# Rotary's quarter swap by ScalarE copies, and x's first block ahead of the other launch loads, in a two-layer decoder trunk

## The chip, the core and the metric

One core of a Trainium2 chip runs the whole program. The metric is device time in microseconds of one execution; the times shown are medians of several executions. TensorE (PE in the views) multiplies, VectorE (DVE) and ScalarE (ACT) do the elementwise work, GpSimd (POOL) some small steps, SyncE (SP) issues most loads. ScalarE and POOL issue DMAs too, in the order of their own instructions.

## The reference

Two layers; each is a token mixer and a gated feed-forward block, both between norms. The mixer has four mLSTM heads and eight attention heads over two key/value heads, 512 positions, window 128. The parts that the change touches are the first norm and the rotary embedding of q and k:

```python
def rmsnorm(x, g):
    xf = x.astype(jnp.float32)
    y = xf * lax.rsqrt(jnp.mean(xf * xf, axis=-1, keepdims=True) + EPS)
    return (y * g.astype(jnp.float32)).astype(x.dtype)

def rope(x):
    ...
    x1, x2 = xf[..., :D // 2], xf[..., D // 2:]
    return jnp.concatenate([x1 * cos - x2 * sin, x2 * cos + x1 * sin], axis=-1)

def reference(...):
    for l in range(DEPTH):
        h = rmsnorm(x, g_pre_mix[l])
        y = token_mixer(h, ...)
        x = x + rmsnorm(y, g_post_mix[l])
        h = rmsnorm(x, g_pre_ffn[l])
        y = conv_ffn(h, ...)
        x = x + rmsnorm(y, g_post_ffn[l])
```

## The kernel before

x is held as four blocks of 128 positions by 1024 channels. Every matrix operand is split into a rounded high part and the rest (`wsplit` L105 and L107 for weights: ScalarE copies the high part, VectorE subtracts; `split_evac` L120 and L121 for results), and each product is three TensorE products (`mm3`, L115).

**Launch.** The first block of x (`xload`, L154) and the constants `cs` with the identity (L656) and weights are issued on SyncE's queue, gb (the norm's gain, one row sent to all 128 partitions, L158) on ScalarE's. `prenorm_a` squares a block on ScalarE with a sum (L166), POOL makes the scale factor (L169, L170), VectorE applies it in two halves (L175). `prenorm_b` transposes the eight 128x128 pieces on TensorE (L183), and ScalarE and VectorE evacuate them, split (L188, L190). `head` then begins the products with the first weights (wta, four units). Engine order at the launch is held by hand: the first weight's split follows the Square of block 0 (`sq[0]`), the second's the evacuation of block 0 (`ev[0]`), the Square of block 1 the same evacuation.

**Attention stage.** Nine channel blocks of 128 (`zchan`, weights wch) are computed channel-major, 24 products each, in the order 4 (k), 1 and 0 (q of the first key/value head, two pairs of heads), 5 (mLSTM), 2 and 3 (q of the second), 6, 7, 8 (mLSTM). "Pair j" below is q's block j. For k and the four q blocks `rotary` runs when the block's PSUM bank is full: ScalarE copies the bank (L364), four DMAs on ScalarE's queue (L368) swap neighbouring quarters of 32 rows, VectorE multiplies the bank by the cosines (L370) and the swapped tile by the sines (`finish`, L373), then adds and splits (L399, L120, L121; for k L389). A `finish` runs inside the next channel block. The mLSTM blocks run a convolution of several VectorE steps (L412, L416).

Between these products, as a `Filler`, run the attention steps for eight pairs of query block and key/value head: scores (`att1`, L470, two PSUM banks), mask and maximum on VectorE (L476, L477, L480), exponentials on ScalarE (L484, L489), normalisation on VectorE (L491 to L493); the transposes of the result (`att2`, L499, one bank), evacuated with a mask by VectorE (L502); the products with v (`att3`, L513). There are four such banks ("aux") and four of "acc". A scheduler of the framework puts the instructions of every engine in one fixed order, by its own estimate of times; each engine works in that order. So a changed duration in the program's text also moves instructions elsewhere.

Of the kernel before, what the change touches and what calls it, by code (L numbers as in the profile page):

```python
# [10 lines left out]
BF16 = mybir.dt.bfloat16  # L11
U16 = mybir.dt.uint16
AF = mybir.ActivationFunctionType
ALU = mybir.AluOpType
# [8 lines left out]

GF = (8, 3, 4, 6)
START = 36
MF = (3, 2, 3, 3, 2)
EPS = 1e-6
NEG = -1e30
# [23 lines left out]
def tile_hymba_trunk(ctx: ExitStack, tc, x, wch, wta, wtb, wout, wup, wdn, par, gv, mhg, cst, rope, out):  # L52
    nc = tc.nc
    NOSYNC = mybir.DependencyInfo(mybir.DependencyClass.NoSync, mybir.DependencyReason.DATA)

    def after(ins, prev):
        if prev is not None:
            tc.add_manual_dep(ins.ins, prev.ins.name, NOSYNC, reason="slots")
        return ins
# [7 lines left out]
    wk = ctx.enter_context(tc.tile_pool(name="wk", bufs=10))  # L67
# [20 lines left out]
    def work(dt=F32):  # L88
        return wk.tile([128, WRK], dt, tag="wk", name=nm("wk"))

    def psum():
        return pp.tile([128, 512], F32, tag="aux", name=nm("aux"))
# [4 lines left out]
    def small(n, tag):  # L97
        return sp.tile([128, n], F32, tag=tag, name=nm(tag), bufs=1 if n >= 16 else 4)
# [52 lines left out]
    xs = [keep.tile([128, D], F32, name=f"x{c}") for c in range(NT)]  # L151

    def xload(c, eng=nc.sync):
        eng.dma_start(xs[c], x[c * 128:(c + 1) * 128, :])  # L154

    def gload(l, i, eng=None, gate=None):
        g = gbp.tile([128, D], F32, tag="gb", name=nm("gb"))
        after((eng or nc.gpsimd).dma_start(g, gv[l, i:i + 1, :].to_broadcast([128, D])), gate)  # L158
        return g

    sq, st, ev = {}, {}, {}

    def prenorm_a(c, gb, gate=None):
        junk = wk.tile([128, 1024], BF16, tag="wk", name=nm("junk"))
        ss = small(1, "ss")
        sq[c] = nc.scalar.activation(junk, xs[c], AF.Square, scale=1.0 / 32, accum_out=ss)  # L166
        after(sq[c], gate)
        rs = small(1, "rs")
        nc.gpsimd.tensor_scalar(rs, ss, EPS, None, ALU.add)  # L169
        nc.gpsimd.tensor_tensor(rs, rs, neghalf[:, 0:1], ALU.pow)  # L170
        hs = []
        for hf in range(2):
            h = work()
            sl = slice(hf * 512, hf * 512 + 512)
            st[c] = nc.vector.scalar_tensor_tensor(h[:, :512], xs[c][:, sl], rs, gb[:, sl], ALU.mult, ALU.mult)  # L175
            hs.append(h)
        return hs
# [182 lines left out]


    def rotary(y, ps, outs):
        r0 = work()
        nc.scalar.activation(r0[:, :512], ps, AF.Copy)  # L364
        r1 = work()
        for b in range(4):
            s = (b ^ 1) * 32
            nc.scalar.dma_start(r1[b * 32:b * 32 + 32, :512], r0[s:s + 32, :512])  # L368
        o = work()
        nc.vector.tensor_tensor(o[:, :512], ps, y.rcos, ALU.mult)  # L370

        def finish():
            nc.vector.tensor_tensor(r1[:, :512], r1[:, :512], y.rsin, ALU.mult)  # L373
            outs(o, r1)
        return finish
# [275 lines left out]

    hT = new_hT(hp)
    hs = {}
    xload(0)
    gb = gload(0, 0, nc.scalar)
    nc.sync.dma_start(cs, cst[:, 0:C_K])  # L656
    hs[0] = prenorm_a(0, gb)
    uA = head_weights(0, (0,), sq[0], st[0])
    prenorm_b(0, hs[0], hT)
    uA += head_weights(0, (1,), ev[0][0], ev[0][1])  # L660
# [22 lines left out]
    for l in range(L):  # L683
# [9 lines left out]
        for i in range(len(its) + 3):  # L693
# [9 lines left out]
            if 0 <= i - 3 < len(its) and its[i - 3][0] % 2:  # L703
                b, kv = its[i - 3]
# [65 lines left out]
        for hf in range(2):  # L770
            for n0 in range(0, 3):
                ps, w = first[seq[n0]]
# [5 lines left out]
        for i in range(2 * NK2):  # L778
            us = []
            for j in (i, i + 2 * NK2):  # L780
                if j in first:
                    ps = first[j][0]
                else:
                    w = upw(j)
                    ps = acc()
# [3 lines left out]
            s = work()  # L789
# [7 lines left out]
            _, lastg = split_evac(s[:, :512], o[0], o[1])  # L797
# [12 lines left out]
        for hf in range(2):  # L810
            if hf:
                banks[1] = [psum() for _ in range(NT)]
            for k2 in range(NK2 - (NTAIL if hf else 0)):
                w, _ = wsplit(wdn[l, hf, k2], 1024, wp)
# [3 lines left out]
        for k2 in range(NK2 - NTAIL, NK2):  # L818
            w, gate = wsplit(wdn[l, 1, k2], 1024, gp, lastg)
# [90 lines left out]
```

## Time and profile before

| | |
|---|---|
| median of 3 runs | 1131.44 us (1131.03 to 1133.36) |
| the profiled execution | 1130.86 us |
| its span, first to last instruction | 1129.1 us |
| TensorE busy | 1108.7 us, 98% |
| VectorE, ScalarE, POOL busy | 659.4, 455.9, 46.7 us |
| DMA | 111.07 MB, mean 98 GB/s |
| chain that ended last, by engine | TensorE 91%, VectorE 2%, DMA 1%, ScalarE 1% |

The span is what the traced instructions take; the execution's own time has 1.8 us more around it. A TensorE instruction's end is modelled, so TensorE's waits are read from the time lines, where a bracket gives the idle time before a row and what ended it.

### The profile page before, as it was taken

Reading aid. Unit: us, or ns where it says so; the run is one execution under the profiler, and the core shown is the slowest. Engines: PE = TensorE matmul, PEld = TensorE weight load, DVE = VectorE, ACT = ScalarE, POOL = GpSimd, SP = SyncE. Lnnn points to the kernel's source line nnn. Section 1 sums busy time; section 2 is a strip of 40 time slices with the busy share of each in tenths; the row PEclk is TensorE's granted clock in tenths of the full one; section 3 lists DMA queues with packets and bytes.
Section 4 is the critical chain, followed back from the end, with each engine's and each line's share of the span. In section 5 each row is a group of like instructions: output and inputs, shape, how many; then the busy total and the mean of one; then the engine's idle time right before and its main releaser. Section 6 shows DMA issues by size and latency. Waiting matters only on the chain.

```text
span 1129.1 us, 14371 instructions
## 1 busy us (share of the span) xinstructions
PE 1108.7 (98%) x5504; PEld 921.1 (82%) x5504; DVE 659.4 (58%) x1094; ACT 455.9 (40%) x882; POOL 46.7 (4%) x106
## 2 busy tenths in 40 slices
PE   6999999999999999999999999999999999999997
PEld 6877788988888888888897777889888888888886
DVE  5588775566666565223557887566566655652223
ACT  5454563444334443223354445444443334431221
POOL 2000011100000000000100000110000000000001
PEclk9999999999999999999999999999999999999999
DMA  7331440233333332334223215202222333233322
GB/s 265 110 98 45 145 135 13 89 112 93 95 101 104 93 93 93 98 108 127 81 93 107 77 62 187 75 19 90 98 94 93 96 102 102 94 93 93 97 90 74
DMA packets 33171, 111.07 MB, mean 98 GB/s; under 512 B 4192, under 2 KB 4352, under 8 KB 33104
## 3 DMA queue, kind: packets, MB, share of 16 engines
q1 hardware_dynamic: 29808, 102.98, 28.7%
q0 software_dynamic: 1232, 4.04, 1.1%
q10 hardware_dynamic: 2064, 3.15, 1.0%
q8 instruction: 43, 0.70, 0.3%
q14 instruction: 24, 0.20, 0.1%
HBM read 104.91 MB, written 2.10 MB: 95 GB/s over the span
## 4 chain that ended last, share of the span: by engine, by line
PE 91%; DVE 2%; DMA 1%; ACT 1%; issue 0%; ACTq 0%; DVEq 0%; POOLq 0%; POOL 0%
PE acc L115 74%; PE aux L115 11%; PE aux L513 1%; DMA wk<-wk 1%; PE aux L183 1%; PE aux L470 1%; PE aux L569 1%; PE aux L499 1%; PE aux L549 0%; DVE wk L412 0%; DVE w L107 0%; DMA raw<-in_wout_dram 0%; ACT wk L484 0%; PE aux L605 0%; PE aux L627 0%
## 5 line engine op out<-in xcount | busy, mean ns | idle before, releaser
L115 PE MATMUL acc<-g,w 128*128 128x512 f32 (+1 forms) x2256 | 482.0, 376 | 0.0
L115 PEld LDWEIGHTS acc<-g,w 128*128 128x128 f32 x2256 | 404.2, 188 | 76.7
L107 DVE TENSOR_TENSOR w<-raw,w 128x1024 fp32r<-128x1024 f32 (+2 forms) x162 | 192.8, 1191 | 267.6 <-ACT w L105 267.5
L105 ACT ACTIVATE w<-raw 128x1024 fp32r<-128x1024 f32 (+2 forms) x162 | 167.7, 1035 | 336.9 <-PE acc L115 294.7
L115 PE MATMUL acc<-w,h 128*128 128x384 f32 (+2 forms) x672 | 146.1, 364 | 0.7 <-DVE h L190 0.5
L648 DVE SCALAR_TENSOR_TENSOR wk<-acc,par,wk 128x511 f32<-128x511 f32 (+1 forms) x176 | 131.3, 746 | 3.0
L115 PEld LDWEIGHTS acc<-w,h 128*128 128x128 f32 x672 | 118.7, 190 | 17.2 <-issue 4.8
L115 PE MATMUL acc<-h,w 128*128 128x512 f32 x432 | 106.4, 398 | 0.0
L115 PEld LDWEIGHTS acc<-h,w 128*128 128x128 f32 x432 | 78.9, 188 | 18.2 <-issue 1.5
L115 PE MATMUL acc<-w,g 128*128 128x512 f32 x384 | 88.7, 389 | 0.0
L115 PEld LDWEIGHTS acc<-w,g 128*128 128x128 f32 x384 | 72.1, 188 | 15.0
L646 ACT ACTIVATE wk<-acc,par 128x512 f32<-128x512 f32 x88 | 58.9, 669 | 0.0
L115 PE MATMUL aux<-g,g 128*128 128x512 f32 x240 | 55.0, 389 | 0.0
L120 ACT ACTIVATE g<-wk 128x512 fp32r<-128x512 f32 x36 | 22.8, 633 | 76.3 <-DVE wk L791 68.3
L115 PEld LDWEIGHTS aux<-g,g 128*128 128x128 f32 x240 | 45.0, 188 | 9.3
L115 PE MATMUL acc<-h,g 128*128 128x512 f32 x192 | 45.2, 393 | 0.1
L115 PE MATMUL aux<-w,h 128*128 128x512 f32 x192 | 43.8, 389 | 0.0
L115 PEld LDWEIGHTS aux<-w,h 128*128 128x128 f32 x192 | 36.0, 188 | 7.5
L115 PEld LDWEIGHTS acc<-h,g 128*128 128x128 f32 x192 | 35.6, 188 | 7.7 <-ACT g L120 0.5
L175 DVE SCALAR_TENSOR_TENSOR wk<-x,rs,gb 128x512 f32<-128x512 f32 x32 | 22.7, 748 | 29.4 <-POOL rs L170 29.4
L203 POOL TENSOR_SCALAR rs<-ss 128x1 f32<-128x1 f32 x16 | 5.7, 358 | 747.0 <-ACT junk L198 747.0
L121 DVE TENSOR_TENSOR g<-wk,g 128x512 fp32r<-128x512 f32 x36 | 24.9, 690 | 18.6 <-ACT g L120 18.6
(172 smaller groups left out, 934.3 us busy)
## 6 DMA issues: line engine op xcount, KB each, us to landing
raw<-in_wup_dram SPq DMA_DIRECT2D x88, 512.0 KB, 3.5
raw<-in_wdn_dram SPq DMA_DIRECT2D x44, 512.0 KB, 3.5
raw<-in_wch_dram SPq DMA_DIRECT2D x18, 512.0 KB, 4.2
raw<-in_wout_dram SPq DMA_DIRECT2D x16, 512.0 KB, 3.6
raw<-in_wtb_dram SPq DMA_DIRECT2D x16, 384.0 KB, 3.0
raw<-in_wta_dram SPq DMA_DIRECT2D x8, 392.0 KB, 4.4
wk<-wk ACTq DMA_DIRECT2D x40, 64.0 KB, 2.1
x<-in_x_dram SPq DMA_DIRECT2D x4, 512.0 KB, 7.3
```

The lines of the kernel that those rows point to most:

```text
L105: i = nc.scalar.activation(hi[:, :n], raw[:, :n], AF.Copy)
L107: after(nc.vector.tensor_tensor(lo[:, :n], raw[:, :n], hi[:, :n].bitcast(F32), ALU.subtract), gate2)
L115: i = nc.tensor.matmul(o, ls[a], rs[b], start=first and n == 0, stop=last and n == 2)
L120: i = nc.scalar.activation(hi, ps, AF.Copy)
L121: return i, nc.vector.tensor_tensor(lo, ps, hi.bitcast(F32), ALU.subtract)
L175: st[c] = nc.vector.scalar_tensor_tensor(h[:, :512], xs[c][:, sl], rs, gb[:, sl], ALU.mult, ALU.mult)
L183: nc.tensor.transpose(ps[:, k * 128:(k + 1) * 128], hs[hf][:, k * 128:(k + 1) * 128], ident)
L470: i = nc.tensor.matmul(pss[p][:, pr, k0:256], q[kv][r, qs], k[r, ks], start=n == 0, stop=n == 2)
L499: nc.tensor.transpose(ps[:, g * 128:(g + 1) * 128], t.P[:, g], ident)
L513: y.lastpv = nc.tensor.matmul(aos[k][64 * p:64 * p + 64, o:o + 256], y.avt[:, t.b - 1 + kh, t.kv * 64:t.kv * 64 + 64], t.PT[:, kh * 512 + ...
L646: nc.scalar.activation(u[:, :512], ps, AF.Copy, scale=cw[:, 2:3])
L648: nc.vector.scalar_tensor_tensor(u[:, d:512], ps[:, 0:512 - d], cw[:, 2 - d:3 - d], u[:, d:512], ALU.mult, ALU.add)
```

## The change

Four edits. (1) The first block of x is loaded as two halves of 512 columns, both ahead of everything else on SyncE's queue; gb moves from ScalarE's queue to SyncE's, behind them. (2) The Square of that block is done by halves, and POOL adds the two sums with the epsilon in one step. (3) Before the first transposes TensorE does 13 products of a tile of zeros, which VectorE has set, into a bank of its own. (4) In `rotary` the copy and the four DMAs become four ScalarE copies of 32 rows, straight from the PSUM bank into the swapped quarters.

```diff
-    def prenorm_a(c, gb, gate=None):
+    def prenorm_a(c, gb, gate=None, halves=False):
         junk = wk.tile([128, 1024], BF16, tag="wk", name=nm("junk"))
-        ss = small(1, "ss")
-        sq[c] = nc.scalar.activation(junk, xs[c], AF.Square, scale=1.0 / 32, accum_out=ss)
-        after(sq[c], gate)
         rs = small(1, "rs")
-        nc.gpsimd.tensor_scalar(rs, ss, EPS, None, ALU.add)
+        if halves:
+            ss = small(2, "ss2")
+            for hf in range(2):
+                sl = slice(hf * 512, hf * 512 + 512)
+                sq[c] = nc.scalar.activation(
+                    junk[:, sl], xs[c][:, sl], AF.Square, scale=1.0 / 32, accum_out=ss[:, hf:hf + 1])
+            nc.gpsimd.tensor_scalar(rs, ss[:, 0:1], ss[:, 1:2], EPS, ALU.add, ALU.add)
+        else:
...
     def rotary(y, ps, outs):
-        r0 = work()
-        nc.scalar.activation(r0[:, :512], ps, AF.Copy)
         r1 = work()
         for b in range(4):
             s = (b ^ 1) * 32
-            nc.scalar.dma_start(r1[b * 32:b * 32 + 32, :512], r0[s:s + 32, :512])
+            nc.scalar.activation(r1[b * 32:b * 32 + 32, :512], ps[s:s + 32, :], AF.Copy)
         o = work()
         nc.vector.tensor_tensor(o[:, :512], ps, y.rcos, ALU.mult)
...
-    xload(0)
-    gb = gload(0, 0, nc.scalar)
+    for hf in range(2):
+        nc.sync.dma_start(xs[0][:, hf * 512:hf * 512 + 512], x[0:128, hf * 512:hf * 512 + 512])
+    gb = gload(0, 0, nc.sync)
     nc.sync.dma_start(cs, cst[:, 0:C_K])
-    hs[0] = prenorm_a(0, gb)
+    wz = wk.tile([128, 1024], BF16, tag="wk", name="wz")
+    nc.vector.memset(wz[:, 0:512], 0.0)
+    wps = psum()
+    for _ in range(WARM):
+        nc.tensor.matmul(wps, wz[:, 0:128], wz[:, 0:512], start=True, stop=True)
+    hs[0] = prenorm_a(0, gb, halves=True)
```

The order of the instructions moves in three places that matter here. Lines are those of the changed file, some two to ten higher: L117 for L115, L376 and L378 for L364 and L370, L381 for L373, L478 for L470, L507 and L510 for L499 and L502, L123 for L121.

SyncE's queue at the launch, before:

```order
L154 DMA x_103<-in_x_dram 128x1024
L656 DMA cs<-in_cst_dram 128x272
L102 DMA raw_129<-in_wta_dram 128x784
L102 DMA raw_153<-in_wta_dram 128x784
L154 DMA x_104<-in_x_dram 128x1024
L102 DMA raw_188<-in_wta_dram 128x784
L154 DMA x_105<-in_x_dram 128x1024
L154 DMA x_106<-in_x_dram 128x1024
L102 DMA raw_195<-in_wta_dram 128x784
```

and with the change:

```order
L663 DMA x_103<-in_x_dram 128x512 x2
L160 DMA gb_117<-in_gv_dram 128x1024
L665 DMA cs<-in_cst_dram 128x272
L104 DMA raw_147<-in_wta_dram 128x784
L104 DMA raw_171<-in_wta_dram 128x784
L156 DMA x_104<-in_x_dram 128x1024
L104 DMA raw_206<-in_wta_dram 128x784
L156 DMA x_105<-in_x_dram 128x1024
L104 DMA raw_213<-in_wta_dram 128x784
L156 DMA x_106<-in_x_dram 128x1024
```

x's first block is now two entries, and gb stands between it and the constants; of the later loads the fourth weight unit has moved in front of the fourth block.

TensorE at the first scores of layer 0, before (acc_638 is pair 2's bank, g_402 and g_403 are k's high and low parts, g_397 and g_399 those of pairs 0 and 1 of q):

```order
L115 MATMUL acc_638<-h_110,w_634 128x512
L470 MATMUL aux_652<-g_402,g_397 128x128
L470 MATMUL aux_653<-g_402,g_397 128x128
L470 MATMUL aux_652<-g_403,g_397 128x128
L470 MATMUL aux_653<-g_403,g_397 128x128
L115 MATMUL acc_638<-h_114,w_634 128x512
L115 MATMUL acc_638<-h_110,w_635 128x512
L115 MATMUL acc_638<-h_110,w_634 128x512
L115 MATMUL acc_638<-h_114,w_634 128x512
L470 MATMUL aux_652<-g_402,g_399 128x128
```

and with the change (bank acc_650, k in g_420 and g_421, q in g_415 and g_417):

```order
L117 MATMUL acc_650<-h_112,w_646 128x512
L117 MATMUL acc_650<-h_108,w_647 128x512
L478 MATMUL aux_664<-g_420,g_415 128x128
L478 MATMUL aux_665<-g_420,g_415 128x128
L478 MATMUL aux_664<-g_421,g_415 128x128
L478 MATMUL aux_665<-g_421,g_415 128x128
L478 MATMUL aux_664<-g_420,g_417 128x128
```

The first score stood behind 19 of pair 2's 24 products; now it stands behind 12, and nothing lies any more between the fourth score and the fifth, the first to need q's low part. Layer 1 has the same two orders.

VectorE in the same stretch, before (wk_578 is pair 0's swapped tile, wk_583 its cosine product, acc_595 block 5's bank):

```order
L370 TENSOR_TENSOR wk_583<-acc_543,g_228 128x512
L399 TENSOR_TENSOR wk_530<-wk_535,wk_530 128x512
L107 TENSOR_TENSOR w_709<-raw_706,w_708 128x1024
L121 TENSOR_TENSOR g_399<-wk_530,g_397 128x512
L121 TENSOR_TENSOR g_403<-g_401,g_402 128x512 x2
L373 TENSOR_TENSOR wk_578<-wk_578,g_228 128x512
L412 SCALAR_TENSOR_TENSOR wk_624<-acc_595,par_222,wk_624 128x511
L399 TENSOR_TENSOR wk_578<-wk_583,wk_578 128x512
L412 SCALAR_TENSOR_TENSOR wk_624<-acc_595,par_222,wk_624 128x510
L107 TENSOR_TENSOR w_794<-raw_791,w_793 128x1024
L121 TENSOR_TENSOR g_399<-wk_578,g_397 128x512
```

and with the change, with what each row waits for (wk_590 is pair 0's swapped tile, wk_595 its cosine product):

```order
L378 TENSOR_TENSOR wk_595<-acc_557,g_246 128x512 [waits PE_49,Activation_49]
L123 TENSOR_TENSOR g_421<-g_419,g_420 128x512 [waits DMASW4_49,Activation_49]
L123 TENSOR_TENSOR g_421<-g_419,g_420 128x512 [waits DMASW5_49,Activation_49]
L381 TENSOR_TENSOR wk_590<-wk_590,g_246 128x512
L109 TENSOR_TENSOR w_719<-raw_716,w_718 128x1024 [waits DMAHW0_49,Activation_49]
L407 TENSOR_TENSOR wk_590<-wk_595,wk_590 128x512 [waits DVE_49]
L109 TENSOR_TENSOR w_802<-raw_799,w_801 128x1024 [waits DMAHW1_49,PE_49,Activation_49]
L420 SCALAR_TENSOR_TENSOR wk_636<-acc_607,par_240,wk_636 128x511 [waits Activation_49]
L123 TENSOR_TENSOR g_417<-wk_590,g_415 128x512 [waits Activation_49]
```

The cosine product L378 waits for ScalarE (Activation), the sine product L381 behind it for nothing of its own; between it and q's low part there are now both weight splits of that stretch.

## Rows read from the trace of the kernel before

**Rows 1.** The page, part 1: busy us (share of span) xinstructions, by engine.

```profile
PE 1108.7 (98%) x5504; PEld 921.1 (82%) x5504; DVE 659.4 (58%) x1094; ACT 455.9 (40%) x882; POOL 46.7 (4%) x106
```

**Rows 2.** Timeline, launch: start us, us, instruction [idle before <-releaser].

```profile
6.07 1.06 ACT L166 ACTIVATE junk<-x 128x1024 bf16<-128x1024 f32 x1 [3.62 <-DMA x<-in_x_dram]
...
6.83 0.23 DVE L135 CAST identb<-cs 128x128 bf16<-128x128 f32 x1 [5.97 <-DMA cs<-in_cst_dram]
...
7.87 0.86 ACT L105 ACTIVATE w<-raw 128x784 fp32r<-128x784 f32 x1 [0.65 <-DMA raw<-in_wta_dram]
...
8.22 1.41 DVE L175 SCALAR_TENSOR_TENSOR wk<-x,rs,gb 128x512 f32<-128x512 f32 x2 [1.16 <-POOL rs L170]
...
9.03 1.97 PE L183 MATMUL aux<-cs,wk 128*128 128x128 f32 x8 [9.03 <-DVE wk L175]
...
10.65 4.45 PE L115 MATMUL acc<-w,h 128*128 128x392 f32 x12
...
11.03 0.66 ACT L188 ACTIVATE h<-aux 128x256 fp32r<-128x256 f32 x2 [0.19 <-PE aux L183]
...
12.32 1.06 ACT L166 ACTIVATE junk<-x 128x1024 bf16<-128x1024 f32 x1
...
28.51 1.04 PE L183 MATMUL aux<-cs,wk 128*128 128x128 f32 x8
```

**Rows 3.** Tile views of x, then of gb: time from issue to landing.

```profile
DMA to landing us min/median/max: 5.3/7.3/8.3
...
DMA to landing us min/median/max: 5.5/5.5/5.5
```

**Rows 4.** Windows: us; PE, PEld, DVE, ACT, POOL busy (x); PEclk, DMA share, GB/s.

```profile
4.00:6.00 2.00, 0.00 (x0) 0.00 (x0) 0.00 (x0) 0.00 (x0) 0.00 (x0) 1.00 0.92 312
...
9.00:11.00 2.00, 1.97 (x9) 1.95 (x10) 1.65 (x3) 0.66 (x2) 0.00 (x0) 1.00 1.05 424
```

**Rows 5.** Timeline of layer 0 around the first scores (L470).

```profile
57.66 1.15 ACT L120 ACTIVATE g<-g 128x512 fp32r<-128x512 f32 x2 [0.57 <-issue]
...
58.32 1.30 DVE L121 TENSOR_TENSOR g<-g,g 128x512 fp32r<-128x512 f32 x2 [0.17 <-ACT g L120]
...
59.65 2.88 PE L115 MATMUL acc<-h,w 128*128 128x512 f32 x12
...
62.05 1.22 DVE L107 TENSOR_TENSOR w<-raw,w 128x1024 fp32r<-128x1024 f32 x1
...
62.46 0.44 PE L470 MATMUL aux<-g,g 64*128 64x128 f32 x4
...
63.19 0.69 DVE L121 TENSOR_TENSOR g<-wk,g 128x512 fp32r<-128x512 f32 x1
```

**Rows 6.** Timeline of TensorE: its waits in the attention stages of layers 0 and 1.

```profile
99.23 0.63 PE L499 MATMUL aux<-cs,wk 128*128 128x128 f32 x4 [1.28 <-DVE g L502]
...
617.46 0.44 PE L470 MATMUL aux<-g,g 64*128 64x128 f32 x4 [1.04 <-ACT g L120]
...
619.18 0.66 PE L470 MATMUL aux<-g,g 64*128 64x128 f32 x8 [0.16 <-DVE g L121]
...
654.37 0.63 PE L499 MATMUL aux<-cs,wk 128*128 128x128 f32 x4 [1.20 <-DVE g L502]
```

**Rows 7.** Windows, layer 0 from the first scores to the wait at 99.23; columns as in rows 4.

```profile
62.46:99.23 36.77, 35.49 (x204) 27.27 (x204) 32.34 (x70) 16.19 (x50) 0.00 (x0) 1.00 0.27 79
```

**Rows 8.** Groups by form, ScalarE, 31 to 130 us: shapes xcount | busy us, mean ns | idle.

```profile
L364 ACT ACTIVATE wk<-acc 128x512 f32<-128x512 f32 x5 | 2.9, 588 | 0.0
...
L410 ACT ACTIVATE wk<-acc,par 128x512 f32<-128x512 f32 x4 | 3.1, 780 | 0.0
...
L489 ACT ACTIVATE den<-es 128x4 f32<-128x4 f32 x8 | 1.7, 214 | 0.0
```

**Rows 9.** Source view of L368: ns min/median/max; waits view: us, times, longest.

```profile
L368 ACTq DMA_DIRECT2D wk<-wk x40: 514/602/1535, 41.8 to 631.6; - x40
...
DVE wk L373 <- DMA wk<-wk: 4.8, 4, 2.0
```

More of the change, by code (lines that the diff above doesn't have):

```diff
@@ L25 @@
 START = 36
+WARM = 13
 MF = (3, 2, 3, 3, 2)
@@ L161, in tile_hymba_trunk @@
     sq, st, ev = {}, {}, {}
-    def prenorm_a(c, gb, gate=None):
+    def prenorm_a(c, gb, gate=None, halves=False):
         junk = wk.tile([128, 1024], BF16, tag="wk", name=nm("junk"))
-        ss = small(1, "ss")
-        sq[c] = nc.scalar.activation(junk, xs[c], AF.Square, scale=1.0 / 32, accum_out=ss)
-        after(sq[c], gate)
         rs = small(1, "rs")
-        nc.gpsimd.tensor_scalar(rs, ss, EPS, None, ALU.add)
+        if halves:
[6 more added lines that the diff above has]
+        else:
+            ss = small(1, "ss")
+            sq[c] = nc.scalar.activation(junk, xs[c], AF.Square, scale=1.0 / 32, accum_out=ss)
+            after(sq[c], gate)
+            nc.gpsimd.tensor_scalar(rs, ss, EPS, None, ALU.add)
         nc.gpsimd.tensor_tensor(rs, rs, neghalf[:, 0:1], ALU.pow)
```

## Prediction

> **What bounds the kernel now.** I read the page's busy shares first: TensorE is busy 1108.7 of 1129.1 us, 98% [rows 1]. A change of a few instructions can therefore win only what TensorE waits for. So the next views are the time lines of the places where it waits: the launch [rows 2] and the attention stage of each layer [rows 5, 6].
>
> In the launch TensorE does nothing for 9.03 us [rows 2]. The chain is to be read off the start times: x's first block is in at 6.07 (Square starts, 1.06 long), VectorE scales it from 8.22, the transposes start at 9.03, ScalarE evacuates the last two quarters of them from 11.03 to 11.69, and only then, behind the split of the second weight unit, the Square of the second block starts at 12.32. Beside this stands a second chain, the first weights: their split starts at 7.87 when their DMA is in.
>
> In the attention stage TensorE stops three times, for 1.20 (1.04 and 0.16), 1.28 and 1.20 us, in all 3.68 [rows 6]. The first waits for ScalarE's and VectorE's split of a rotary result (layer 1 only; in layer 0 TensorE comes to the same scores at 62.46 without a wait [rows 5]), the other two for VectorE's L502, which gives back a PSUM bank. VectorE is the loaded engine there: 32.34 of 36.77 us [rows 7]. So what decides is VectorE's order and what its next instruction waits for.
>
> **The launch, step by step.** x's first block and gb are issued together from two queues and land together, 5.3 and 5.5 us after it [rows 3]. The core moved 312 GB/s meanwhile [rows 4]. If x's two halves (0.52 MB) go first on one queue and gb (0.52 MB) after them, x is in 0.52/0.312 = 1.7 us sooner, at 4.3, and gb where it was, near 6.2.
>
> [...]
>
> The half Squares end near 5.0. The scale factor reached VectorE 1.1 us after the Square's end (7.13 to 8.22), so scaling starts at 6.2. The identity lands at 6.83 as before [rows 2] (the same bytes are ahead of it), so the transposes start near 7.0 instead of 9.03. That is not yet the gain: the evacuation stands behind the first weights' split in ScalarE's order, and this stays at 7.87 to 8.73, the same 1.2 MB being ahead of its load. Four evacuations of 0.33 then end at 10.05 instead of 11.69: 1.6 us sooner. The Square of the second block moves with them; the third block's, at 13.4, can move less, since 3.4 MB have to be in for it. I take **-1.35**; bounds -1.8, and -0.3 if x's halves land only near 6.
>
> The 13 products of zeros cost nothing: at the slow pace (12 products of 392 columns took 4.45 us, waits included [rows 2], so at most 0.48 for 512) they need at most 6.3 us, from about 1.1 on; their cover is TensorE's idle time to 7.0 and, beyond it, the evacuation's wait to 8.73. [...] The second POOL operand and the second accumulator read are a tenth or two, behind gb.
>
> **The rotary, step by step.** Ten times, five a layer. Removed: a 128x512 copy of 0.588 us [rows 8] and four DMAs, which ScalarE issues at 0.60 each [rows 9]. Added: four 32x512 copies. No row shows a 32-row copy. The nearest ScalarE rows bound it: 0.214 for a tiny operand and 0.780 for 512 columns with a table scale [rows 8]; I take the 0.588 of the same columns from the same bank, since the removed copy differs in rows alone, and 0.53 when back to back (two splits took 1.15 [rows 5]): 2.1 us for four. ScalarE itself is held less (2.1 against 0.6 + 2.4), and the swapped tile is ready sooner, by the DMAs' way.
>
> The price is elsewhere. VectorE's cosine product (L378 in the change) waits for ScalarE's last read of the bank, as L370 did; now that is the fourth copy, 1.5 us later, and all that stands behind it in VectorE's order waits too. And the scheduler, counting on the quicker swap, has moved the first scores in front of seven products (12 instead of 19 products of their channel done, 7 x 0.24 = 1.7 us [rows 5]; 12 took 2.88). So I follow the operand that comes last, the low half of q's pair 0 (L123), in the old time scale of layer 0, from pair 1's products ending at 47.0:
>
> - ScalarE: a weight split to 48.0, pair 1's copies to 50.1, table load and gate exponent at 51.7. VectorE: decay copies, sine product, nT, sum end at 53.5. ScalarE splits at 54.1, then copies pair 0 to 56.2 and splits k's two halves to 57.2.
> - VectorE: cosine product 56.8, k's two low halves to 58.0 (they ended at 59.6 [rows 5]), sine product 0.6, a weight's low half 1.15 (62.05 to 63.19 [rows 5]), sum 0.6 (60.3), a second one 1.15, a convolution step 0.65 (62.1), low half of q 62.7.
>
> Before, that low half ended at 63.88 [rows 5]; it is about 1.1 us sooner, but wanted 1.7 us sooner. TensorE comes to the scores at 60.8, waits 0.3 for the high half (split at 61.0), does four, and waits for 62.8: **1.75 us of waits where layer 0 had none and layer 1 had 1.20**.
>
> Behind it VectorE runs on with more holes: in pair 2 and pair 3 its cosine, sine and sum now queue behind the four copies (about 1.2 us each, between the softmax steps that waited already). The L502 pair of the third block, behind which TensorE went on at 99.23 [rows 6], ends near 100.2 by the same walk; TensorE reaches the transposes it frees at about 99.0: **1.15 us**. Together 2.9 us a layer, 5.8 against 3.68: **+2.1**.
>
> **Sum.** -1.35 + 2.1 = +0.75. The profiled execution took 1130.86 (span 1129.1), so 1131.6 on its scale; it lies 0.58 under the median of the runs, 1131.44, which gives **1132.2**. A measurement of this kernel can tell 0.2% from no change, 2.26 us: 1129.2 to 1133.7.
>
> **Rivals.**
>
> *The stalls vanish (faster).* Four times, 4.8 us in all, VectorE's sine product itself waited for the DMAs [rows 9]; if the swap without DMA lets VectorE run ahead everywhere, all 3.68 go: -1.35 - 3.7 = -5.0, 1126.4. For it: VectorE is the bound and loses waits. Against: its order puts two weight splits ahead of q's low half. It would take copies at the lower bound: 4 x 0.2 us. Half of it, the scores' wait staying and the later one going: -1.35 + 3.5 - 3.7 = -1.5, 1129.9.
>
> *The copies hold the bank longer (slower).* At the upper bound, 0.73 each back to back, four take 2.9 us; the cosine product and what stands behind it come 0.8 later in each of the four pairs ahead of the stalls. Two of them lie ahead of the scores (+1.6, none hidden), two ahead of L502; about 1.5 a layer is left after what the softmax waits absorb: 2 x 4.4 - 3.7 - 1.35 = +3.8, 1135.2. It decides from a copy of about 0.65 on, where the median passes 1133.7.
>
> *The launch gives nothing.* x's halves share the engines with gb and the weights behind them and land near 6: -0.3 + 2.1 = +1.8, 1133.2.
>
> **How the numbers follow.** Forecast 0.42, half of the first rival 0.20, its whole 0.17, longer copies 0.12, launch without gain 0.09. Faster by over 2.26: the whole first rival and the better third of its half, 0.24. Slower by over 2.26: longer copies, and the upper parts of the forecast and of the launch rival, 0.19. Same: 0.57. The range 1127.2 to 1134.8 leaves out the better part of the whole first rival and half of the longer copies', together under 0.2.
>
> **What would show it.** Right: the first transposes near 7.0, the Square of the second block near 10.9; zeros over before 7.5. Four copies of some 0.58 with VectorE's L378 starting just behind the fourth. TensorE waiting at the first scores in both layers, about 1.4 to 2 us in all, in two pieces, the second for VectorE's L123; and some 1.2 at the transposes that wait for L510. Wrong: no wait at the scores (then q's low half came a microsecond or more sooner than by my walk), a copy far from 0.58, or a Square of the first block that still starts at 6.

## The result, and the profile after the change

The changed kernel takes 1143.59 us (median of three runs, 1142.80 to 1144.18) against 1131.32 for the kernel before: a ratio of 1.0105, 95% interval 1.0089 to 1.0120. A fourth run took 2734.84 us and is left out; with it the median is 1143.88, the 1143.9 from which some expectations below start. The change is slower by 12.3 us, where 1132.2 was forecast and 1134.8 was the upper end of the range. The profiled execution took 1144.18, its span 1141.5.

The page, part 1, of the changed kernel (as [rows 1]):

```profile
PE 1120.3 (98%) x5517; PEld 927.1 (81%) x5517; DVE 661.2 (58%) x1095; ACT 475.3 (42%) x914; POOL 46.4 (4%) x106
```

TensorE is busy 11.6 us longer for 13 instructions more. These are the zeros, which take 5.3 us of what was idle time (the first row of the time line below); the other 6.3 us are the products of before, made slower by something that the windows below show. So about half of the loss stands in the page as busy time. The waits view names the idle part (TensorE; us in total, times, longest):

```profile
PE aux L193 <- DVE wk L185: 3.9, 3, 3.0
PE aux L507 <- DVE g L510: 3.4, 2, 1.8
PE aux L478 <- ACT g L122: 2.5, 2, 1.2
PE aux L478 <- DVE g L123: 2.5, 2, 1.2
```

The first row is the launch. The other three are the attention stages: 8.4 us, 4.2 a layer, against 3.68 for both before [rows 6]. The time line shows both places (TensorE, ScalarE and VectorE; start us, us, instruction [idle before <-releaser]):

```profile
1.18 5.29 PE L670 MATMUL aux<-wz 128*128 128x512 bf16 x13 [1.18 <-DVE mb L331]
...
3.71 0.63 ACT L172 ACTIVATE junk<-x 128x512 bf16<-128x512 f32 x1 [1.71 <-DMA x<-in_x_dram]
...
8.56 0.23 DVE L137 CAST identb<-cs 128x128 bf16<-128x128 f32 x1 [7.42 <-DMA cs<-in_cst_dram]
8.70 1.41 DVE L185 SCALAR_TENSOR_TENSOR wk<-x,rs,gb 128x512 f32<-128x512 f32 x2
...
9.50 1.97 PE L193 MATMUL aux<-cs,wk 128*128 128x128 f32 x8 [3.04 <-DVE wk L185]
...
9.69 0.86 ACT L107 ACTIVATE w<-raw 128x784 fp32r<-128x784 f32 x1 [4.62 <-DMA raw<-in_wta_dram]
...
54.88 2.39 ACT L376 ACTIVATE wk<-acc 32x512 f32<-32x512 f32 x4
...
57.30 0.69 DVE L378 TENSOR_TENSOR wk<-acc,g 128x512 f32<-128x512 f32 x1 [1.73 <-ACT wk L376]
...
59.17 0.69 DVE L381 TENSOR_TENSOR wk<-wk,g 128x512 f32<-128x512 f32 x1
...
62.38 0.44 PE L478 MATMUL aux<-g,g 64*128 64x128 f32 x4 [1.25 <-ACT g L122]
...
63.31 0.69 DVE L123 TENSOR_TENSOR g<-wk,g 128x512 fp32r<-128x512 f32 x1
...
64.05 1.11 PE L478 MATMUL aux<-g,g 64*128 64x128 f32 x8 [1.23 <-DVE g L123]
65.09 9.04 PE L117 MATMUL acc<-h,w 128*128 128x512 f32 x27
...
104.77 0.63 PE L507 MATMUL aux<-cs,wk 128*128 128x128 f32 x4 [1.67 <-DVE g L510]
```

In the launch x is in sooner (Square at 3.71, not 6.07), but the identity (8.56, not 6.83) and the first weights (9.69, not 7.87) come later [rows 2], and the transposes start 0.5 later than before. Part of that is SyncE's issuing, one entry after another: the constants now stand behind two more entries, of 0.40 and 0.43 us. Before, and with the change:

```profile
1.17 0.42 SPq L656 DMA_DIRECT2D cs<-in_cst_dram  x1
```

```profile
2.11 0.43 SPq L665 DMA_DIRECT2D cs<-in_cst_dram  x1
```

So 0.9 of the identity's 1.7 us are lost before its transfer begins, and the rest from issue to landing (6.4 us, 5.6 before). In layer 0 TensorE waits 1.25 and 1.23 at the first scores, and then 27 products take 9.04, 0.335 each, where 16 took 3.92, 0.245 each, in the same place before:

```profile
64.53 3.92 PE L115 MATMUL acc<-h,w 128*128 128x512 f32 x16
```

The windows of the changed kernel show why (columns as in [rows 4]):

```profile
0.00:10.00 10.00, 5.79 (x16) 2.23 (x17) 1.73 (x5) 2.95 (x6) 1.36 (x12) 0.96 0.76 247
10.00:20.00 10.00, 8.55 (x44) 7.11 (x44) 8.04 (x16) 8.00 (x18) 3.39 (x6) 0.86 0.76 268
60.00:70.00 10.00, 7.52 (x29) 5.66 (x29) 8.80 (x17) 3.99 (x13) 0.00 (x0) 0.70 0.28 92
620.00:630.00 10.00, 7.52 (x30) 5.69 (x29) 8.90 (x18) 4.41 (x13) 0.00 (x0) 0.68 0.30 93
50.65:127.92 77.27, 73.13 (x407) 57.81 (x405) 61.18 (x133) 40.72 (x115) 0.00 (x0) 0.96 0.20 62
611.06:688.20 77.14, 72.88 (x407) 57.67 (x405) 61.18 (x133) 40.75 (x115) 0.00 (x0) 0.96 0.19 62
```

In windows of 1 us the granted clock behind the 0.70 of layer 0 is 0.95 from 63 to 64 us, 0.50 in each from 64 to 70 and 0.63 from 70 to 71, and behind the 0.68 of layer 1 it is 0.85 from 623 to 624, 0.50 in each from 624 to 630 and 0.74 from 630 to 631. So the fall begins inside the second of the two waits in both layers; here two waits of 1.2 us stand ahead of it, and the work behind them starts slow (27 products in 9.04 and, in layer 1, 8.75).

The first two rows hold a fall too: windows of 1 us put it from 9.3 to 12.7 us (0.65 from 9 to 10, 0.50 to 12, 0.65 from 12 to 13), behind the 3.04 us of idle time between the zeros and the transposes. The eight transposes lie inside it.

The last two rows cut one stretch out of each layer, from the transpose of nT to the end of the mask product of the seventh of the eight units (block and kv head). The same stretch before, and the first ten us:

```profile
0.00:10.00 10.00, 0.97 (x5) 0.97 (x6) 2.07 (x5) 3.29 (x4) 1.28 (x12) 1.00 0.78 285
```

```profile
50.46:121.18 70.72, 69.44 (x407) 55.34 (x405) 61.44 (x134) 33.51 (x103) 0.29 (x1) 1.00 0.30 86
604.34:676.29 71.95, 69.54 (x407) 55.31 (x405) 61.54 (x133) 33.50 (x103) 0.45 (x1) 1.00 0.28 84
```

VectorE's busy time in it is the same (61.2 to 61.5 us); the stretch is 6.55 and 5.19 us longer, 11.7 of the 12.4 us between the spans. So VectorE's **idle time**, length less VectorE's busy time, is the quantity to follow: 9.3 and 10.4 before, 16.1 and 16.0 after. With the work fixed this is only another way to write the stretch's length; what makes VectorE idle is the question. VectorE's waits from 40 to 112 us have a first row that the kernel before has not:

```profile
DVE wk L378 <- ACT wk L376: 7.5, 5, 3.1
DVE rd L499 <- ACT den L497: 4.6, 5, 1.5
```

Five cosine products waited 7.5 us for the four copies. A copy takes what was forecast (ScalarE's groups by form, 31 to 130 us; x, total, mean ns):

```profile
L376 ACT ACTIVATE wk<-acc 32x512 f32<-32x512 f32 x20 | 11.8, 590 | 2.1 <-PE acc L117 1.8
```

### The profile page after: what moved, and what is told of

Its sections match the earlier page's. It is cut to its first block, busy times and chain, and to the rows that moved or that the text cites. A ratio compares the mean times of both kernels' runs of the same rounds, so it can differ in the third digit from the quotient of the medians.

```text
span 1141.5 us, 14355 instructions
## 1 busy us (share of the span) xinstructions
PE 1120.3 (98%) x5517; PEld 927.1 (81%) x5517; DVE 661.2 (58%) x1095; ACT 475.3 (42%) x914; POOL 46.4 (4%) x106
## 4 chain that ended last, share of the span: by engine, by line
PE 90%; DVE 4%; ACT 3%; DMA 2%; issue 1%; POOL 0%; SPq 0%; DVEq 0%; POOLq 0%; ACTq 0%
PE acc L117 73%; PE aux L117 10%; PE aux L521 1%; ACT wk L376 1%; PE aux L193 1%; PE aux L478 1%; DVE w L109 1%; PE aux L577 1%; DMA cs<-in_cst_dram 1%; PE aux L507 1%; DMA g<-in_cst_dram 1%; DVE wk L420 0%; PE aux L557 0%; DMA raw<-in_wch_dram 0%; ACT wk L492 0%
## 5 line engine op out<-in xcount | busy, mean ns | idle before, releaser
L117 PE MATMUL acc<-g,w 128*128 128x512 f32 (+1 forms) x2256 | 482.0, 376 | 0.0
L117 PEld LDWEIGHTS acc<-g,w 128*128 128x128 f32 x2256 | 404.2, 188 | 76.7
L117 PE MATMUL acc<-w,h 128*128 128x384 f32 (+2 forms) x672 | 145.7, 363 | 0.8 <-DVE w L109 0.5
L117 PEld LDWEIGHTS acc<-w,h 128*128 128x128 f32 x672 | 118.0, 189 | 17.5 <-issue 5.6
L117 PE MATMUL acc<-h,w 128*128 128x512 f32 x432 | 110.8, 411 | 0.0
L117 PEld LDWEIGHTS acc<-h,w 128*128 128x128 f32 x432 | 82.7, 196 | 19.8 <-issue 1.5
L117 PE MATMUL acc<-w,g 128*128 128x512 f32 x384 | 88.7, 389 | 0.0
L117 PEld LDWEIGHTS acc<-w,g 128*128 128x128 f32 x384 | 72.1, 188 | 15.0
L117 PE MATMUL aux<-g,g 128*128 128x512 f32 x240 | 55.0, 389 | 0.0
L117 PEld LDWEIGHTS aux<-g,g 128*128 128x128 f32 x240 | 45.0, 188 | 9.3
L117 PE MATMUL acc<-h,g 128*128 128x512 f32 x192 | 45.2, 393 | 0.1
L117 PE MATMUL aux<-w,h 128*128 128x512 f32 x192 | 43.8, 389 | 0.0
L117 PEld LDWEIGHTS aux<-w,h 128*128 128x128 f32 x192 | 36.0, 188 | 7.5
L117 PEld LDWEIGHTS acc<-h,g 128*128 128x128 f32 x192 | 35.6, 188 | 7.7 <-ACT g L122 0.5
L123 DVE TENSOR_TENSOR g<-wk,g 128x512 fp32r<-128x512 f32 x36 | 24.9, 692 | 19.9 <-ACT g L122 19.7
```

What stands on the lines that cost most here:

```text
L117: i = nc.tensor.matmul(o, ls[a], rs[b], start=first and n == 0, stop=last and n == 2)
L123: return i, nc.vector.tensor_tensor(lo, ps, hi.bitcast(F32), ALU.subtract)
```

## The experiments

**Which half of the change.** The diff of the first run undoes the edit of `rotary` (shown in part); that of the second undoes all others.

```diff
+        r0 = work()
+        nc.scalar.activation(r0[:, :512], ps, AF.Copy)
...
-            nc.scalar.activation(r1[b * 32:b * 32 + 32, :512], ps[s:s + 32, :], AF.Copy)
+            nc.scalar.dma_start(r1[b * 32:b * 32 + 32, :512], r0[s:s + 32, :512])
```

> The launch of the change with the rotary of before. Theory (all of the loss comes from the rotary: two waits at the first scores, and TensorE's clock falling to its lower level behind them): 1131.3 + 0.2 = 1131.5 us, scores without long waits, granted clock 1.00 from 30 us on. Rival (the launch, whose weights, gb and identity land later, carries a quarter of the loss): 1134 or more.

Measured: 1130.64 us, ratio 0.9995 (0.9986 to 1.0005).

> The rotary of the change with the launch of before. Theory: 1143.6 us; two waits of 1.2 at the first scores in each layer, granted clock near 0.70 in the ten us that follow them, some 1.7 at the transposes behind them. Rival (the launch carries a quarter): 1140.

Measured: 1141.24 us, ratio 1.0098 (1.0079 to 1.0118). Its windows:

```profile
60.00:70.00 10.00, 7.21 (x32) 5.45 (x32) 8.82 (x18) 4.72 (x14) 0.00 (x0) 0.83 0.30 92
50.87:127.12 76.25, 71.70 (x407) 56.71 (x405) 61.14 (x133) 40.71 (x115) 0.00 (x0) 0.98 0.20 62
610.45:686.31 75.86, 71.64 (x407) 56.67 (x405) 61.14 (x133) 40.71 (x115) 0.00 (x0) 0.98 0.20 63
```

The launch costs nothing that can be measured; the rotary alone costs 10.1 us by the medians, between the theory's number and the rival's. Together they cost 12.3, but the two intervals (1.0079 to 1.0118 and 1.0089 to 1.0120) overlap. In the profiled executions the rows show a fall of the clock of half the length here (0.83 in the ten us, not 0.70) and 1.0 to 1.3 us less in each stretch. Of the four runs of the rotary alone, three took 1140.3 to 1141.6 us at a mean granted clock of 0.996, one 1145.4 at 0.992. A mean that is 0.004 lower over 1139 us is an estimated 4.6 us of clock, about what that run is longer by. So the clock's loss varies between runs of one kernel, and goes with the time; what decides it isn't settled.

**The clock or VectorE.** If the fall of the clock is a cause, keeping TensorE busy through the waits should win it back.

```diff
+FILLZ = 20
...
+    zk = keep.tile([128, 128], BF16, name="zk")
+    nc.gpsimd.memset(zk, 0.0)
...
+                if b == 0 and kv == 0 and pr == 0 and n in (0, 2):
+                    for _ in range(FILLZ):
+                        z = nc.tensor.matmul(pss[0][:, 0, k0:256], zk, zk, start=n == 0, stop=n == 0)
+                        if n == 0:
+                            after(z, newest[0])
```

> The whole change, and in each layer 20 products of zeros (128 columns) ahead of the first score and 20 more, added into the open sums, ahead of the first score that reads q's low half: TensorE is busy where it waited, the scores start when they did. Theory (the fall of the clock behind the two waits costs 2.9 us a layer by itself): granted clock 1.00 through the attention stage and 1143.9 - 5.8 = 1138.1 us. Rival (the clock falls for another cause, or its fall costs nothing because VectorE is behind anyway): 1143.9, or the clock still at 0.70.

Measured: 1144.48 us, ratio 1.0118 (1.0103 to 1.0134). Layer 1's stretch, and TensorE's time line in it:

```profile
612.53:689.40 76.87, 72.82 (x447) 57.93 (x445) 61.23 (x133) 40.48 (x115) 0.00 (x0) 1.00 0.20 62
```

```profile
650.52 1.12 PE L486 MATMUL aux<-g,g 64*128 64x256 f32 x12 [1.33 <-DVE es L504]
663.58 0.76 PE L118 MATMUL acc<-w,h 128*128 128x384 f32 x3 [0.74 <-DVE wk L423]
666.23 0.63 PE L515 MATMUL aux<-cs,wk 128*128 128x128 f32 x4 [1.89 <-DVE g L518]
```

The clock stayed at 1.00 in all of layer 1's stretch, and the stretch is no shorter than the change's by more than 0.3 us (76.87 to 77.14). What the clock no longer takes comes back in waits for VectorE at 650 to 666 us. (In layer 0 the clock fell all the same, 0.83 from 100 to 110 us, and the ten products behind a wait of 1.88 at 105 us took 3.33 in place of the change's 1.99.) This is the rival's number, and my first theory, that the fall costs 2.9 us a layer by itself, found no support. The run isn't a clean measure of the fall, though: the scheduler also put one convolution step of VectorE ahead of the first softmax, and the stretch of layer 1 is 1.0 us longer than in the run with the rotary alone.

```diff
-START = 36
+START = 40
```

> The whole change with START 40 in place of 36: 12 more products (2.9 us) ahead of the first scores. Theory: both waits at the scores and the fall of the clock go, 2 x (2.5 + 2.9) = 10.8 us less: 1133.1 us, with the waits at the transposes as they were. Rival (VectorE is behind by then, and the waits move on to the softmax and the transposes): 1139 or more.

Measured: 1140.20 us, ratio 1.0082 (1.0065 to 1.0099). The two longest waits of TensorE in layer 1:

```profile
639.07 0.98 PE L478 MATMUL aux<-g,g 64*128 64x256 f32 x11 [1.44 <-DVE g L510]
661.50 0.77 PE L117 MATMUL acc<-w,h 128*128 128x384 f32 x3 [1.14 <-DVE wk L420]
```

The first scores aren't waited for, no wait is over 1.44 and the clock doesn't fall in either stage (1.00 in both stretches), but four waits for VectorE and ScalarE (two more of 0.63 and 0.33) have come in their place. Some 3.4 us came back, not 10.8. This is the rival's case: moving TensorE's work about wins only a part. VectorE's order moved with it, so what the order itself does isn't separated here.

**What holds VectorE.** Three ways to swap the quarters without VectorE waiting for four copies out of the bank.

```diff
+        o = work()
+        nc.vector.tensor_tensor(o[:, :512], ps, y.rcos, ALU.mult)
         r1 = work()
         for b in range(4):
...
-        o = work()
-        nc.vector.tensor_tensor(o[:, :512], ps, y.rcos, ALU.mult)
```

> The whole change, with VectorE's cosine product written ahead of the four copies, so that the copies wait for it and it waits for nothing. Theory 2 (the stage's length is set by VectorE, whose cosine product waited 1.5 us for the copies five times in each layer; TensorE's waits and its clock only show it): VectorE's waits for the copies gone, TensorE's waits at the scores and the transposes near those of before, and some 11 to 12 us less than the change: 1132 us. Rival (ScalarE's 2.4 us for the copies make the splits late by themselves): 1138 us or more, with TensorE still waiting over 2 us at the first scores.

Measured: 1138.86 us, ratio 1.0062 (1.0042 to 1.0083). VectorE's longer waits from 40 to 112 us, and TensorE's (the profiled execution took 1142.58, the slowest of the five, so its waits may be longer than the median run's):

```profile
DVE wk L381 <- ACT wk L378: 3.7, 5, 1.1
DVE g L123 <- ACT g L122: 1.7, 3, 0.8
```

```profile
PE aux L507 <- DVE g L510: 5.6, 2, 2.8
```

The cosine product no longer waits for the copies, and the scores aren't waited for; but now the sine product waits for the copies (3.7) and the low halves for ScalarE's splits (1.7), and TensorE's wait has moved to the transposes, 2.8 in one piece, with a fall of the clock (0.98 and 0.96 in the stretches; the ten products behind the wait took 3.06 and 3.55, in place of the change's 1.99 and 2.01). Some five of the 12.3 us came back, not eleven: the time is the rival's, though its sign, waits at the first scores, is missing. The wait for the bank was only a part of it.

```diff
+        r0 = work()
+        nc.scalar.activation(r0[:, :512], ps, AF.Copy)
...
-            nc.scalar.activation(r1[b * 32:b * 32 + 32, :512], ps[s:s + 32, :], AF.Copy)
+            nc.scalar.activation(r1[b * 32:b * 32 + 32, :512], r0[s:s + 32, :512], AF.Copy)
```

> The whole change, with one 128-row copy out of the bank as before and then the four 32-row copies from that copy, all on ScalarE: the bank is free after 0.59 us, ScalarE is held for 3.0 us in place of 2.4. Theory 2 (the bank held for four copies): VectorE's cosine product waits little and the time falls by some 9 us to 1135. Rival (ScalarE's time): 0.6 us more in each of ten rotaries, 1146 or more.

Measured: 1142.80 us, ratio 1.0085 (1.0064 to 1.0106). Neither number came: the bank is free early, and the sine product waits for the fourth copy instead, 5.8 us in five times (40 to 112 us). It looks as if the gain of the one and the 0.63 us of a further copy nearly cancel.

```diff
-            nc.scalar.activation(r1[b * 32:b * 32 + 32, :512], r0[s:s + 32, :512], AF.Copy)
+            nc.gpsimd.tensor_copy(r1[b * 32:b * 32 + 32, :512], r0[s:s + 32, :512])
```

> The whole change, with one 128-row copy out of the bank on ScalarE and the four 32-row copies from it on GpSimd. Theory 2: VectorE's cosine product waits for nothing; what is left is how soon GpSimd has the swapped rows: 1131 if a copy takes under 0.8 us, 1138 if it takes 2. Rival (ScalarE's time is the cause): 1131 in any case, since ScalarE is back at one copy.

Measured: 1144.84 us, ratio 1.0103 (1.0081 to 1.0126). The source view of these copies:

```profile
L378 POOL COPY wk<-wk x40: 604/628/1692, 42.0 to 643.6; 32x512 f32<-32x512 f32 x40
...
  DVE wk L383: 12.8, 10
```

Neither number came. ScalarE is back at one copy, and the loss is all there; a GpSimd copy takes 0.63 in the median, under the 0.8 at which I expected 1131, but four of them take 2.66 to 4.07 us (40 to 110 us), and the sine product waits 12.8 us in all. So it is not ScalarE's time and not the bank alone; what these three runs have in common is that the swapped rows are late for VectorE, on whichever engine.

Late means late for the place that VectorE's order gives them. In the kernel before they come later still: from the start of pair 0's copying to its sine product there are 6.0 us, against 4.3 with the change. These are the rows before:

```profile
53.56 0.58 ACT L364 ACTIVATE wk<-acc 128x512 f32<-128x512 f32 x1
...
59.53 0.69 DVE L373 TENSOR_TENSOR wk<-wk,g 128x512 f32<-128x512 f32 x1
```

There other steps of VectorE stand between, and one copy alone holds the bank.

**The copies' length by itself.** One copy, then two and three, in place of four:

```diff
-        for b in range(4):
-            s = (b ^ 1) * 32
-            nc.scalar.activation(r1[b * 32:b * 32 + 32, :512], ps[s:s + 32, :], AF.Copy)
+        nc.scalar.activation(r1[:, :512], ps, AF.Copy)
```

> The whole change with one 128-row copy out of the bank in place of the four: the swap of row quarters is left out, so the rotary's second term reads unswapped rows. Theory 3 (VectorE does the same 61.2 us of work up to the fourth block's mask products in every kernel so far, and the stage lasts that long plus VectorE's idle time; the idle time comes from how long the four copies take): a copy of 0.59 in place of 2.4 takes the idle time from 16 us a layer to 10 or less, and the time to 1130. Rival (the scheduler's order, made for a quicker swap, loses the time whatever the copies take): idle time stays above 13, 1138 or more.

(The unit that this text calls the fourth block is the stretch's seventh unit.) Measured: 1131.00 us, ratio 1.0000 (0.9991 to 1.0009).

```profile
50.32:121.12 70.80, 69.29 (x407) 55.45 (x405) 60.86 (x131) 33.21 (x103) 0.00 (x0) 1.00 0.21 67
604.15:674.93 70.78, 69.22 (x407) 55.41 (x405) 60.88 (x131) 33.20 (x103) 0.00 (x0) 1.00 0.22 67
```

```profile
97.07 0.63 PE L505 MATMUL aux<-cs,wk 128*128 128x128 f32 x4 [1.20 <-DVE g L508]
```

The theory's number came, and its idle time (9.9 us a layer). The last row is TensorE's one long wait in layer 0's stretch.

```diff
+        nc.scalar.activation(r1[0:64, :512], ps[64:128, :], AF.Copy)
+        nc.scalar.activation(r1[64:128, :512], ps[0:64, :], AF.Copy)
```

> The whole change with two copies of 64 rows in place of four of 32: halves are swapped instead of quarters, so the rotary's second term reads other rows. VectorE's order in layer 0's attention stage is that of the run with one copy, instruction for instruction, so only the copies' time differs: 1.2 us in place of 0.6. If the loss grows with every copy alike (1143.9 - 1131.0 over 1.8 us): 1135.3 us, idle time of VectorE 12 us a layer. If the stage has slack for a copy more: 1131 to 1132, with the scores not waited for. If a copy's time depends on its rows: longer than 0.59 each.

Measured: 1136.37 us, ratio 1.0039 (1.0025 to 1.0052). This is the number for a loss with every copy. A window, and TensorE's one wait in layer 0's stretch:

```profile
49.75:123.28 73.53, 70.72 (x407) 56.84 (x405) 61.56 (x131) 35.72 (x107) 0.00 (x0) 0.98 0.20 65
```

```profile
98.30 0.63 PE L506 MATMUL aux<-cs,wk 128*128 128x128 f32 x4 [2.81 <-DVE g L509]
```

```diff
+        nc.scalar.activation(r1[0:32, :512], ps[32:64, :], AF.Copy)
+        nc.scalar.activation(r1[32:64, :512], ps[0:32, :], AF.Copy)
+        nc.scalar.activation(r1[64:128, :512], ps[64:128, :], AF.Copy)
```

> The same with three copies (two of 32 rows, one of 64, whose quarters are not swapped): 1.8 us. If the loss grows with every copy alike: 1139.6 us, idle time 14 us a layer. If there is slack and then a steep step, where TensorE's waits at the first scores come close together and its clock falls: under 1135 here, and the larger part of the loss between three copies and four.

Measured: 1136.93 us, ratio 1.0036 (1.0020 to 1.0052); stretches of 74.70 and 74.02. Neither number came.

| copies | held, us | time, us | VectorE's idle time a layer | TensorE's clock in the stretch |
|---|---|---|---|---|
| 1 | 0.59 | 1131.0 | 9.9, 9.9 | 1.00 |
| 2 | 1.19 | 1136.4 | 12.0, 12.0 | 0.98 |
| 3 | 1.77 | 1136.9 | 12.9, 12.4 | 0.98 |
| 4 | 2.4 | 1143.6 | 16.1, 16.0 | 0.96 |

The times are medians; idle time and clock are those of the profiled executions (1130.3, 1134.6, 1137.7 and 1144.2 us).

The step from one copy to two is the clean one. VectorE's order in both stretches is the same, only a copy of 0.59 is added, and 5.4 us are lost: TensorE's wait at the transposes grows from 1.2 to 2.8, and the clock falls behind it (ten products in 3.45 in place of 2.01; 0.98 in the stretch in place of 1.00). The loss doesn't grow evenly: there is one step where the wait at the transposes gets long, and one where the two waits at the first scores reach 1.2 each. The second, from three copies to four, isn't the copies' length alone, since VectorE's order changes there too. One copy puts the scores where the change has them, in front of the seven products, and loses nothing: the scheduler's moving them forward was not a cause by itself. And its 1131.0 says that a swap at the cost of a single copy would only have drawn level.

**Work taken off VectorE, and the launch's queue.**

```diff
-            nc.vector.tensor_tensor(r1[:, :512], r1[:, :512], y.rsin, ALU.mult)
+            nc.gpsimd.tensor_tensor(r1[:, :512], r1[:, :512], y.rsin, ALU.mult)
```

> The kernel before, with the rotary's sine product on GpSimd in place of VectorE. Theory 3 (VectorE's work and idle time set the stage's length): VectorE has 5 x 0.69 = 3.4 us less work a layer and doesn't wait for the DMAs itself, so most of TensorE's 3.7 us of waits go: 1128 us. Rival (GpSimd's product takes 2 us or more, and the sum behind it waits for that): 1131 or more.

Measured: 1141.13 us, ratio 1.0087 (1.0073 to 1.0100). The rival by mechanism, though GpSimd's product takes 1.3 to 1.6 us, not 2: VectorE has less to do and idles more (15.8 and 16.3 us a layer). TensorE waits 4.9 us, 2.5 in one piece, for the split of the rotary's result at the first scores, and its clock falls in both layers (0.95 and 0.96 in the stretch). The scheduler put the scores three products earlier here too. This fits the reading that lateness in the rotary's chain counts, whoever causes it.

```diff
-    gb = gload(0, 0, nc.sync)
+    gb = gload(0, 0, nc.scalar)
```

> The launch of the change with gb issued from ScalarE's queue as before, and the rotary of before. Theory for the launch (with everything on SP's queue the identity landed at about 9.0 in place of 6.8 and the first weights' split started at 10.0 in place of 7.9, which ate what x's halves had won): the identity near 7, the split near 8, the first transposes near 7.5 to 8, and some 1 us less than the launch of the change: 1129.7 us. Rival (the queue makes no difference, the engines are shared anyway): identity and split near 9 and 10 again, 1130.6.

Measured: 1130.43 us, ratio 0.9989 (0.9980 to 0.9998). Its time line:

```profile
5.50 0.63 ACT L172 ACTIVATE junk<-x 128x512 bf16<-128x512 f32 x1 [3.04 <-DMA x<-in_x_dram]
...
6.92 0.23 DVE L137 CAST identb<-cs 128x128 bf16<-128x128 f32 x1 [5.79 <-DMA cs<-in_cst_dram]
...
7.90 0.86 ACT L107 ACTIVATE w<-raw 128x784 fp32r<-128x784 f32 x1 [0.65 <-DMA raw<-in_wta_dram]
9.14 1.97 PE L193 MATMUL aux<-cs,wk 128*128 128x128 f32 x8 [2.99 <-DVE wk L185]
```

With gb on a second queue the identity and the first weights are back at 6.9 and 7.9, and x's halves are in at 5.5 and 6.5 rather than 3.7 and 4.3: the transposes start at 9.14, as before. The theory's identity and split came, its transposes and its 1129.7 did not: the queue moves the lateness from one load to another. No version here is faster than the kernel before by more than this one's 0.11%.

## Why the prediction was wrong, by its own steps

**The launch: the step that failed is "the identity lands at 6.83 as before (the same bytes are ahead of it)".** In place of -1.35 the launch alone measured -0.5, with an interval of -1.6 to +0.6 that the time alone can't narrow; the rows decide. The halves of x did better than forecast (in at 3.7, not 4.3; half Squares over at 5.0). But the identity and the first weights came 1.7 and 1.8 us later, the split not at 7.87 but at 9.69, and so the transposes at 9.50, not 7.0. VectorE has the identity's cast ahead of the scaling, so an early x couldn't help. The bytes ahead were the same; the issue times and the queues were not (2.11 instead of 1.17 for the constants). The core moved 247 GB/s in the first ten us against 285. That x's halves, first in one queue, get the whole 312 GB/s and are in 1.7 us sooner, on which the -1.35 rests, was my estimate: no row before shows one queue alone at the start, and no run shows a gain of 1.35. With the change the first half was in 2.36 us sooner, the identity 1.73 later; that nothing behind x would be later didn't follow from the estimate. The launch rival had the size, a gain of 0.3, but not the reason: x's halves didn't land near 6.

**The zeros: nothing speaks against their costing nothing.** The eight transposes took 1.97 us with them and without, at a granted clock of 0.50 from 9.5 us on with the change and of 1.00 before [rows 4]; so the view's clock doesn't account for their pace. No run leaves out the zeros alone.

**The copies: right for one, short for four.** 0.590 us each against 0.588, but 2.4 for four against 2.1 (back to back they don't get shorter: 0.60 each).

**The walk to the first scores: right in kind, short in size.** TensorE came to the scores at 61.1 (forecast 60.8), the second cosine product ended at 58.0 (56.8) and q's low half at 64.0 (62.7), all by the rows above; two waits in both layers, 1.25 and 1.23, where 1.75 in all was forecast (the walk's own steps give 1.6: from 60.8 to 62.8, less 0.4 for the four scores).

**The step that failed: "together 2.9 us a layer, 5.8 against 3.68: +2.1".** Layer 0's terms measured 2.48 at the scores and 1.67 at the transposes (forecast 1.15), 4.15. Two more terms were missing: the 27 products behind the scores took 9.04, and the same 27 took 6.39 in the run with the cosine first and 6.39 in the run with one copy, whose granted clock is 1.00 in the whole stretch, so the fall of the clock shows as 2.6; and the eight scores took 1.11 instead of 0.66. That makes 7.2 us for layer 0 in place of 2.9. I had the view that shows the level of the clock, and never asked what two waits so close together would do to it.

Behind this lies a deeper error, to which the experiments with zeros and with more products point: I costed TensorE's waits one by one, as if each were a hole to be filled. VectorE's idle time grew, by 6 us a layer, with its work unchanged; TensorE shows that as waits and as a slow clock, and where an experiment closed one wait, others opened. "About 1.2 us each, between the softmax steps that waited already" was taken as hidden; the softmax steps waited no less afterwards (4.6 against 4.4 us).

**The rivals.** The stalls didn't vanish. The longer-copies rival had the direction and the place, but not the condition: it was to decide from a copy of 0.65 on, and the copies were 0.59. Its 1135.2 was still 8.4 too low.

What stays open: how much of the loss is the clock's own. By TensorE's account its longer waits (8.4 against 3.7 us) and the time that the two falls take (an estimated 3.4 us each, what the clock is short of 1.00 in the windows of 1 us, added up) make 11.5 of the 12.4 us between the spans, yet the run whose zeros kept the clock up in layer 1 won nothing there. Open too is why the parts (-0.5 and +10.1) fall short of the whole by some 3 us, which is within what the intervals allow. And an obvious rival was not run: the four copies in the instruction order of the kernel before. The order here was made by the scheduler's own estimate of the copies, so part of the loss may be the order's; nor were the scores moved forward in the kernel before with nothing else changed.

## What to carry to other kernels

Where two engines work into each other in order, follow the loaded engine's work and idle time over the whole stage and not the waits of the engine that is nearly always busy: a later operand can cost its lateness each time, and filling the hole on the other engine can just move it. Before trading DMAs for copies, ask how late the last operand is by each way and who stands behind it; here a copy of 32 rows took 0.590 us and one of 128 rows 0.591, so four of 32 cost as much as four of 128 would. And when a wait on TensorE grows past those that the trace already has, price what the clock does behind it: here 2.8 us in place of 1.2 went with 0.98 in place of 1.00 over a stretch of 73.5 us.

## What the runs showed of the hardware that I had not expected

- A ScalarE copy of 512 columns out of a PSUM bank took the same for 32, 64 and 128 rows: 0.590, 0.592 to 0.596 and 0.591 us. Split by rows into four, the copy took 2.4 us in place of 0.59.
- In the attention stages of these traces TensorE kept its pace behind single waits of up to 1.78 us (behind those of 1.67 to 1.78 ten products took 1.99 to 2.01). Behind waits of 1.88 to 1.94 it slowed in four cases of six, in the runs with zeros and with the copies from SBUF or by GpSimd (ten products in 3.29 to 3.45, or 27 in 7.81 in place of 6.42; by GpSimd another wait of 0.58 came four scores later). Every stretch with a wait of 2.4 to 3.3 had a mean granted clock of 0.95 to 0.98, and where the time lines show the ten products behind that wait they took 2.71 to 3.55. Two waits of 1.23 to 1.55 with four scores between them also had a fall behind them, in both layers of the change and of the rotary alone (27 products in 8.00 to 9.04); two of 0.65 and 1.35 did not (6.42 and 6.43). Four windows of ten us that hold such a fall (the change's two, the rotary alone's and the one with zeros, in layer 0) read 0.68 to 0.83; windows of 1 us in the change read 0.50 at the lowest.
- The same loads from one queue (the change and the launch alone) and from two (gb on ScalarE's): x's first half in at 3.71 and 3.48, and at 5.50; the identity at 8.56 and 9.03, and at 6.92.
